# Alternating the forgetting and stick-breaking head pairs of a hybrid block on one Trainium2 core

## The chip, the core and the metric

One of the eight cores of a Trainium2 chip. The time is the device time of one execution in microseconds; several executions are timed and the median is taken. The engines are named as the profile names them: PE (TensorE; PEld its weight loads), DVE (VectorE), ACT (ScalarE), POOL (GpSimd) and SP (SyncE, whose queue issues most of the DMAs here).

## What is computed

Two transformer blocks on one sequence of 512 tokens (528 with 16 meta tokens), model width 1024, float32. The change lies in the mixer of the first block. Cut to it:

```python
proj = xn @ w_in[layer]
q_a, k_a, v_a, f_a, q_b, k_b, v_b, g_a, g_b = jnp.split(proj, SPLIT_POINTS, axis=-1)
log_f = jax.nn.log_sigmoid(f_a + b_forget[layer])
o_a = forgetting_attention(q_a, k_a, v_a, log_f)      # softmax(q k^T / 8 + c[t] - c[s]), c = cumsum(log f)
o_b = stick_breaking_attention(q_b, k_b, v_b)         # exp(log_sigmoid(z) + later), s < t
y_a = merge(o_a) @ w_o_fox[layer]
y_b = merge(o_b) @ w_o_sb[layer]
mixed = (jax.nn.sigmoid(g_a) * y_a + jax.nn.sigmoid(g_b) * y_b) @ w_out[layer]
h = h + rms_norm(mixed, norm_gains[layer, 1])
```

Here `later` is the sum of log_sigmoid(-z) over the keys between s and t, taken as a reversed cumulative sum. Each of the two attentions has eight heads of width 64; they are worked on in pairs, four pairs of either kind. Then come the first block's feed-forward part and a second block, whose ada rows (`silu(c) @ w_ada`) are already begun in the first mixer.

## The kernel before, in words

Every float32 product is made of three matmuls: both operands are split in a high and a low part of type fp32r, and `mm3` (L95 to L106) adds high × high (L102), low × high (L105) and high × low (L106). A weight tile is 128 × 512 (256 KB): SP loads it (`wr`), ACT copies it to its high part `wh` (L90), DVE subtracts to get the low part `wl` (L91). `dense` runs one weight key's column tile of 128 columns over the sequence in two halves (about 258 or 264 columns); a tile over 8 k tiles takes 48 matmuls, one over 4 takes 24.

`attention(fam, pr, pf)` is one pair, fam 0 forgetting, fam 1 stick-breaking. It projects q, k and v (three column tiles of `w_qkv`, 144 matmuls), forms scores in five query blocks (block 0 of 2 rows, blocks 4 to 1 of 128; L388 to L394), and turns them into weights P. For a forgetting pair that is a maximum on DVE and one Exp on ACT per block (`fox_rows`). For a stick-breaking pair ACT copies the scores to P (L400), and `sb_rows` runs a chain per block in a wide buffer `sb_l`: Abs, Exp and Ln on ACT, L565 on DVE (max and add), two reversed scans on DVE (L568), a subtraction on DVE (L569), and Exp on ACT. Then PE transposes P (L411), ACT and DVE split the transposed piece (`pt_h` L73, `pt_l` L74), and three matmuls add it to the bank `o` (L418 to L420). The meta keys go through `ptm` (L426 to L436). A forgetting pair divides by its sums (`rt` transposes L445, `rs` L449 to L452); both kinds are split to `o_h`, `o_l`.

The order of work: the program gives all instructions in one order, and a scheduler with a modelled timeline sets from it the order on each engine. Buffers and their numbers decide how far work can run ahead: the weight buffers (4 and 6), two P of each block, two `sb_l`, three banks for scores, one bank for `o`. In the program the forgetting pairs 0 to 3 come first, each followed by two column tiles of the gate projection `w_g` (`gate_a`). Then Silu of the condition, its store by SP, Sigmoid over all eight gated tiles `ya` (L501) and the table load that sets ACT back to Exp and Ln (L502). Then stick-breaking pairs 0 to 3 with no, one, one and six column tiles of `w_of` (the forgetting output projection, `out_a`, 24 matmuls each) behind them. Behind the pairs come eight gate tiles more (`sg`) with two ada rows each (`ada`: SP loads `wa`, 512 KB, L812; DVE multiplies it with the condition `wc` and sums, L813; `wc` itself is loaded at L802 from the stored condition), then `out_b` (`w_os`, L536 multiplies with the gate, POOL adds, the sum is split to `mix_h` and `mix_l`), whose first halves meet the `w_out` projection of the next stage.

Of the kernel before, what the change touches and what calls it, by code (L numbers as in the profile page):

```python
# [19 lines left out]
NT = 528  # L20
# [18 lines left out]
class Kernel:  # L39
# [21 lines left out]
        (eng or self.G).dma_start(out=t, in_=self.A[key])  # L61
        return t

    def load_r(self, p, key, shape, eng=None, dma=None):

        raw = self.load(p, key, shape, dma)
        t = p.tile(shape, F32R, name=key + "r", tag=key + "r")
        (eng or self.G).tensor_copy(t, raw)
        return t

    def split(self, h, l, src, scale=None, eng=None):
# [109 lines left out]
    def run(self):  # L181
        tc, nc = self.tc, self.nc
        top = ExitStack()
        nc.scalar.preload_act_table_set("natural_log_exp_and_others")
        const = self.const = self.pool(top, "const", side="left")
        self.wp = self.pool(top, "wp", bufs=4, side="left")
        self.wq = self.pool(top, "wq", bufs=6, side="left")
        self.gains1 = const.tile([128, 4, 8], F32, name="gains1")
        nc.sync.dma_start(out=self.gains1, in_=self.A["gains1"])
        self.ident = self.load(const, "ident", [128, 128])  # L190
        self.ones = const.tile([128, 1], F32, name="ones")
        self.V.memset(self.ones, 1.0)
        self.c15 = const.tile([128, 1], F32, name="c15")
        self.V.memset(self.c15, 1.5)
        self.zero = const.tile([128, 1], F32, name="zero")
        self.V.memset(self.zero, 0.0)
        self.gains2 = self.load(const, "gains2", [128, 3, 8])
        self.convw = self.load(const, "convw", [128, 44, 4])
        self.b_ada = self.load(const, "b_ada", [128, 48])
        self.mod = const.tile([128, 48], F32, name="mod")  # L200
        self.cond = self.load(const, "cT", [128, 8])
        self.cond_out = self.pool(top, "pdr", space=bass.MemoryType.DRAM).tile([128, 8], F32, name="cond")
        self.n_ada = 0
        xp = self.pool(top, "xp", side="left")
        self.xres = xp.tile([128, 8, NQ], F32, name="xres")
        self.x = self.xres[:, :, 2:NQ]
        self.block1_mixer()
        self.block1_ffn()
        self.block2_mixer()
        self.block2_ffn()  # L210
        top.close()


    def block1_mixer(self):
# [89 lines left out]
        def attention(fam, pr, pf):  # L304
# [59 lines left out]
            vtm = pa.tile([128, 2, 16], F32, tag="vtm", name="vtm")  # L364
            G.tensor_copy(vtm, vt[:, 0:16].unsqueeze(1).to_broadcast([128, 2, 16]))
            tr(tm, vtm.rearrange("p e s -> p (e s)"), ident)
            vmf = pa.tile([32, 128], F32, tag="vmf", name="vmf")
            V.tensor_tensor(vmf, tm, bmask, op=ALU.mult)
            for r in (0, 32):
                act(vm[z][r:r + 32], vmf, AF.Copy)  # L370
# [7 lines left out]
            for b in (0, 4, 3, 2, 1):  # L378
                t0, qn = QB[b]
                n = 16 + 128 * b  # L380
                qs = slice(t0 - T0, t0 - T0 + qn)
                pieces = [(0, n)] if n <= 512 else [(0, 264), (264, 264)]
                for e in range(2):
                    pss = []
                    for c0, cn in pieces:
                        ps = ps_s.tile([128, 512], F32, tag="s", name="s")[0:qn, 0:cn]
                        keys = ks[e][:, c0:c0 + cn]
                        mm(ps, qhh[e][:, qs], keys, start=True, stop=False)  # L388
                        if c0 + cn == n:
                            if b == 0:  # L390
                                mm(ps, self.ident_r[:, 0:2], mr[:, 128:144], start=False, stop=False)
                            else:
                                mm(ps[:, cn - 128:cn], self.ident_r, mr[:, 0:128], start=False, stop=False)
                        mm(ps, qll[e][:, qs], ks2[e][:, c0:c0 + cn], start=False, stop=True)  # L394
                        pss.append((ps, c0, cn))
                    if fam == 0:
                        self.fox_rows(pa2, pss, P[b], e, b, qn, sums)
                    else:
                        for ps, c0, cn in pss:
                            act(P[b][:, e, c0:c0 + cn], ps, AF.Copy)  # L400
                if fam == 1:
                    self.sb_rows(pf, P[b], qn, n)

            o = ps_o.tile([128, 512], F32, tag="o", name="o")
            first = True
# [31 lines left out]
            if fam == 0:  # L437
# [7 lines left out]
                    tr(rt[:, 128 * b - 128:128 * b], rx[:, b, :], ident)  # L445
                rt0 = ps_t.tile([128, 512], F32, tag="t", name="rt0")[:, 0:2]
                tr(rt0, rx[0:2, 0, :], ident[0:2, 0:2])
                rs = pf["pool"].tile([128, NQ], F32, tag="rs", name="rs")
                act(rs[:, 2:NQ], rt, AF.Copy)  # L449
                act(rs[:, 0:2], rt0, AF.Copy)  # L450
                V.tensor_tensor(rs[:, 2:NQ], o, rs[:, 2:NQ], op=ALU.mult)
# [11 lines left out]
        c8 = kc[1]  # L463
        G.memset(c8[0:64].bitcast(F32), 0.0)
        y = pa.tile([8, NT], F32, tag="vt", name="fy")
        l = pf.tile([8, NT], F32, tag="rs", name="fl")
        late = []
        dense("w_f", 0, xn_h, xn_l, 0, KD,
              lambda ps, c0, n: V.tensor_tensor(y[:, c0:c0 + n], ps[0:8], rb[0:8, c0:c0 + n], op=ALU.mult),
# [20 lines left out]
        def out_a(ps, c0, n, i):  # L490
            V.tensor_tensor(ya[:, i, c0:c0 + n], ps, ya[:, i, c0:c0 + n], op=ALU.mult)

        for pr in range(4):
            attention(0, pr, fox)
            for i in (2 * pr, 2 * pr + 1):
                dense("w_g", i, xn_h, xn_l, T0, QD, lambda ps, c0, n: gate_a(ps, c0, n, i))
        self.dump("o0", o_h[0])
        esf.close()
        self.tc.keep_in_program_order(act(self.cond, self.cond, AF.Silu))
        nc.sync.dma_start(out=self.cond_out, in_=self.cond)  # L500
        act(ya, ya, AF.Sigmoid)  # L501
        tables = nc.scalar.preload_act_table_set("natural_log_exp_and_others")  # L502
        self.tc.keep_in_program_order(tables)


        ess = ExitStack()
        psb = self.pool(ess, "psb", bufs=2)
        sb = {"pool": psb, "tables": tables.ins}
        for pr in range(4):
            attention(1, pr, sb)  # L510
            for i in [[], [0], [1], range(2, 8)][pr]:
                dense("w_of", i, o_h[0], o_l[0], 0, QD, lambda ps, c0, n: out_a(ps, c0, n, i))
        self.dump("o1", o_h[1])
        ess.close()
        esa.close()
        esp.close()

# [36 lines left out]
            self.act(P[:, e, c0:c0 + cn], ps, AF.Exp, bias=nm[0:qn, 0:1], accum_out=s2[0:qn, i:i + 1])  # L554
        V.tensor_tensor(sums[0:qn, e, b:b + 1], s2[0:qn, 0:1], s2[0:qn, 1:2], op=ALU.add)

    def sb_rows(self, pf, P, qn, n):

        V, act = self.V, self.act
        l = pf["pool"].tile([128, 2, NT], F32, tag="sb_l", name="sb_l")[0:qn, :, 0:n]  # L560
        with self.tc.issue_after(pf["tables"]):
            act(l, P, AF.Abs)
            act(l, l, AF.Exp, scale=-1.0)
            act(l, l, AF.Ln, bias=self.ones[0:qn])
        V.scalar_tensor_tensor(l, P, 0.0, l, op0=ALU.max, op1=ALU.add)  # L565
        for e in range(2):
            r = l[:, e, ::-1]
            V.tensor_tensor_scan(r, r, self.zero[0:qn].to_broadcast([qn, n]), 0.0, op0=ALU.add, op1=ALU.add)  # L568
        V.tensor_tensor(P, P, l, op=ALU.subtract)  # L569
        act(P, P, AF.Exp)  # L570
# [249 lines left out]
    def block2_mixer(self):  # L820
# [7 lines left out]
        nm = py.tile([128, S], F32R, name="nm")  # L828
        ut = py.tile([128, 4, 36], F32, name="ut")
        fl = py.tile([128, 2, 4, 4], F32, name="fl")  # L830
        sel = self.load_r(py, "lsel", [128, 8], dma=nc.sync)
        mk = [self.load(py, f"lmask{d}", [128, 128], nc.sync) for d in range(2)]
        ng = self.load(py, "mng", [128, 4], nc.sync)
        pcv = self.pool(es_c, "pcv", side="left")
# [618 lines left out]
```

## Time and profile before

| what | value |
|---|---|
| runs | 1557.49, 1564.07, 1560.18 us; median 1560.18 us |
| profiled execution | 1563.27 us, its span 1561.5 us |
| mean granted clock of TensorE | 0.982 |
| PE, DVE, ACT, POOL busy | 96%, 66%, 53%, 11% of the span |
| instructions in the span | 27525 |
| first mixer's head pairs | from about 50 to 370 us of the span |

How to read it: an engine is busy while it executes an instruction; the granted clock is the share of full speed that TensorE was given, so a busy us at 0.5 does half a us of full-speed work. Starts and ends are us from the start of the span. In a timeline the bracket behind a row holds the idle time of that engine just before it and the instruction whose end released it. The span is 1.8 us shorter than the time of the same execution.

### The profile page before, as it was taken

What the parts mean: (1) busy time and instruction counts of PE and PEld (TensorE: products, weight loads), DVE (VectorE), ACT (ScalarE), POOL (GpSimd) and SP (SyncE); (2) the same over time, 40 slices, a digit from 0 to 9 for tenths busy, and PEclk for the clock granted to TensorE, in tenths of its full rate; (3) what the DMA queues carried; (4) which work ended last, traced back from release to release, by engine and by line L of the source; (5) the groups of instructions that cost most, each with busy time, mean ns of one, the idle gap of its engine ahead of it and who ended that gap; (6) DMA issues with size and microseconds to landing.
All of it is one profiled execution on the core that took longest, in us unless ns stands there. A gap on an engine that the chain in (4) does not pass through costs nothing. (4 is left out here: it accounts for less than half of the span.)

```text
span 1561.5 us, 27525 instructions
## 1 busy us (share of the span) xinstructions
PE 1499.8 (96%) x10219; PEld 1366.8 (88%) x10219; DVE 1031.0 (66%) x2052; ACT 821.0 (53%) x1704; POOL 177.6 (11%) x290
## 2 busy tenths in 40 slices
PE   7999998999899899999999999999998999999997
PEld 6999997889899899999899997775788888888887
DVE  7666568875978997787546877656878633333335
ACT  5455667774367654444345666767455433333232
POOL 4000000000234200000002213321331000000000
PEclk9999998999999999999999999999999999999998
DMA  6322232114864544444556653210135633333334
GB/s 190 93 75 86 62 95 75 48 55 143 278 218 139 172 147 139 138 136 121 180 162 173 188 178 116 68 55 0 36 122 177 215 95 95 95 94 88 93 101 138
DMA packets 101510, 190.43 MB, mean 122 GB/s; under 512 B 12480, under 2 KB 19840, under 8 KB 101376
## 3 DMA queue, kind: packets, MB, share of 16 engines
q1 hardware_dynamic: 100432, 187.26, 38.9%
q0 software_dynamic: 944, 1.41, 0.4%
q8 instruction: 80, 1.31, 0.4%
q14 instruction: 54, 0.44, 0.1%
HBM read 181.63 MB, written 2.10 MB: 118 GB/s over the span
## 5 line engine op out<-in xcount | busy, mean ns | idle before, releaser
L91 DVE TENSOR_TENSOR wl<-wr,wh 128x512 fp32r<-128x512 f32 x576 | 401.8, 703 | 285.2 <-ACT wh L90 274.3
L90 ACT ACTIVATE wh<-wr 128x512 fp32r<-128x512 f32 x576 | 355.8, 621 | 437.1 <-PE d L105 312.0
L102 PE MATMUL d<-x_h,wh 128*128 128x258 f32 (+1 forms) x704 | 198.5, 282 | 1.8 <-DVE ev L676 1.7
L106 PE MATMUL d<-x_h,wl 128*128 128x258 f32 (+1 forms) x704 | 198.2, 282 | 0.8 <-DVE wl L91 0.8
L105 PE MATMUL d<-x_l,wh 128*128 128x258 f32 (+1 forms) x704 | 198.8, 283 | 0.0
L102 PE MATMUL d<-xn_h,wh 128*128 128x264 f32 (+2 forms) x656 | 189.4, 290 | 8.2 <-ACT xn_h L247 6.4
L105 PE MATMUL d<-xn_l,wh 128*128 128x264 f32 (+2 forms) x656 | 189.6, 289 | 1.8 <-DVE xn_l L248 1.8
L106 PE MATMUL d<-xn_h,wl 128*128 128x264 f32 (+2 forms) x656 | 189.2, 289 | 0.0
L106 PE MATMUL d<-g_h,wl 128*128 128x256 f32 (+1 forms) x506 | 163.8, 324 | 0.0
L102 PE MATMUL d<-g_h,wh 128*128 128x256 f32 (+1 forms) x506 | 163.6, 323 | 0.0
L105 PE MATMUL d<-g_l,wh 128*128 128x256 f32 (+1 forms) x506 | 163.5, 323 | 0.0
L105 PE MATMUL d<-f_l,wh 128*128 128x512 f32 (+1 forms) x416 | 149.4, 363 | 2.9 <-DVE f_l L796 2.9
L106 PE MATMUL d<-f_h,wl 128*128 128x512 f32 (+1 forms) x416 | 149.1, 362 | 0.0
L102 PE MATMUL d<-f_h,wh 128*128 128x512 f32 (+1 forms) x416 | 146.6, 361 | 1.5 <-ACT f_h L795 1.0
L102 PEld LDWEIGHTS d<-x_h,wh 128*128 128x128 f32 x704 | 132.9, 189 | 2.6 <-DVE ev L676 2.3
L102 PEld LDWEIGHTS d<-xn_h,wh 128*128 128x128 f32 x656 | 125.8, 193 | 9.3 <-ACT xn_h L247 6.7
L106 PEld LDWEIGHTS d<-x_h,wl 128*128 128x128 f32 x704 | 132.8, 189 | 1.0 <-DVE wl L91 1.0
L105 PEld LDWEIGHTS d<-x_l,wh 128*128 128x128 f32 x704 | 132.6, 189 | 0.1
L105 PEld LDWEIGHTS d<-xn_l,wh 128*128 128x128 f32 x656 | 126.1, 192 | 3.3 <-DVE xn_l L248 3.1
L106 PEld LDWEIGHTS d<-xn_h,wl 128*128 128x128 f32 x656 | 126.0, 192 | 0.5 <-DVE wl L91 0.2
L105 PEld LDWEIGHTS d<-g_l,wh 128*128 128x128 f32 x506 | 95.0, 188 | 8.6
L102 PEld LDWEIGHTS d<-g_h,wh 128*128 128x128 f32 x506 | 95.1, 188 | 8.1
(514 smaller groups left out, 3298.2 us busy)
## 6 DMA issues: line engine op xcount, KB each, us to landing
wr<-in_w_down SPq DMA_DIRECT2D x115, 256.0 KB, 2.8
wr<-in_w_up SPq DMA_DIRECT2D x104, 256.0 KB, 2.7
wr<-in_w_gu SPq DMA_DIRECT2D x104, 256.0 KB, 2.6
wa<-in_w_ada SPq DMA_DIRECT2D x48, 512.0 KB, 4.5
wr<-in_w_in SPq DMA_DIRECT2D x68, 256.0 KB, 2.9
wr<-in_w_out SPq DMA_DIRECT2D x56, 256.0 KB, 2.9
wr<-in_w_qkv SPq DMA_DIRECT2D x48, 256.0 KB, 2.7
wr<-in_w_g SPq DMA_DIRECT2D x32, 256.0 KB, 2.6
```

The lines of the kernel that those rows point to most:

```text
L90: self.act(wh, raw, AF.Copy)
L91: eng.tensor_tensor(wl, raw, wh.bitcast(F32), op=ALU.subtract)
L102: m = self.mm(ps, wh[:, k, :], h, start=(j == 0 and k == 0), stop=False)
L105: self.mm(ps, wh[:, k, :], xl[:, k0 + k, c0:c0 + n], start=False, stop=False)
L106: self.mm(ps, wl[:, k, :], h, start=False, stop=(j == last and k == kt - 1))
```

## The change

The two kinds of pair take turns: forgetting 0, stick-breaking 0, forgetting 1 and so on. The gate tiles of `ya` stand behind the stick-breaking pairs, three, three, two and none. All eight `w_of` tiles come behind the last pair. Silu, the store of the condition, Sigmoid and the table load stand between forgetting pair 3 and stick-breaking pair 3. So that both kinds' buffers fit at once, the pool of the wide buffer has two tags of one buffer (528 wide for blocks 4 and 2, 400 wide for the others) in place of two equal ones, and `vmf`, `rs` and `l` are put into other tiles. `load_r` has POOL's queue load straight into the fp32r tile, with no raw tile and no cast. The table set that the program begins with now serves the stick-breaking pairs up to the third.

```diff
--- before.py
+++ after.py
@@ -61,11 +61,10 @@
         (eng or self.G).dma_start(out=t, in_=self.A[key])
         return t
 
-    def load_r(self, p, key, shape, eng=None, dma=None):
-
-        raw = self.load(p, key, shape, dma)
+    def load_r(self, p, key, shape):
+
         t = p.tile(shape, F32R, name=key + "r", tag=key + "r")
-        (eng or self.G).tensor_copy(t, raw)
+        self.G.dma_start(out=t, in_=self.A[key])
         return t
 
     def split(self, h, l, src, scale=None, eng=None):
@@ -181,7 +180,7 @@
     def run(self):
         tc, nc = self.tc, self.nc
         top = ExitStack()
-        nc.scalar.preload_act_table_set("natural_log_exp_and_others")
+        self.tables = nc.scalar.preload_act_table_set("natural_log_exp_and_others")
         const = self.const = self.pool(top, "const", side="left")
         self.wp = self.pool(top, "wp", bufs=4, side="left")
         self.wq = self.pool(top, "wq", bufs=6, side="left")
@@ -364,7 +363,7 @@
             vtm = pa.tile([128, 2, 16], F32, tag="vtm", name="vtm")
             G.tensor_copy(vtm, vt[:, 0:16].unsqueeze(1).to_broadcast([128, 2, 16]))
             tr(tm, vtm.rearrange("p e s -> p (e s)"), ident)
-            vmf = pa.tile([32, 128], F32, tag="vmf", name="vmf")
+            vmf = vt[0:32, 16:144]
             V.tensor_tensor(vmf, tm, bmask, op=ALU.mult)
             for r in (0, 32):
                 act(vm[z][r:r + 32], vmf, AF.Copy)
@@ -399,7 +398,7 @@
                         for ps, c0, cn in pss:
                             act(P[b][:, e, c0:c0 + cn], ps, AF.Copy)
                 if fam == 1:
-                    self.sb_rows(pf, P[b], qn, n)
+                    self.sb_rows(pf, P[b], b, qn, n)
 
             o = ps_o.tile([128, 512], F32, tag="o", name="o")
             first = True
@@ -445,7 +444,7 @@
                     tr(rt[:, 128 * b - 128:128 * b], rx[:, b, :], ident)
                 rt0 = ps_t.tile([128, 512], F32, tag="t", name="rt0")[:, 0:2]
                 tr(rt0, rx[0:2, 0, :], ident[0:2, 0:2])
-                rs = pf["pool"].tile([128, NQ], F32, tag="rs", name="rs")
+                rs = pa2.tile([128, NT], F32, tag="pt_h", name="rs")[:, 0:NQ]
                 act(rs[:, 2:NQ], rt, AF.Copy)
                 act(rs[:, 0:2], rt0, AF.Copy)
                 V.tensor_tensor(rs[:, 2:NQ], o, rs[:, 2:NQ], op=ALU.mult)
@@ -463,7 +462,7 @@
         c8 = kc[1]
         G.memset(c8[0:64].bitcast(F32), 0.0)
         y = pa.tile([8, NT], F32, tag="vt", name="fy")
-        l = pf.tile([8, NT], F32, tag="rs", name="fl")
+        l = pa2.tile([8, NT], F32, tag="pt_h", name="fl")
         late = []
         dense("w_f", 0, xn_h, xn_l, 0, KD,
               lambda ps, c0, n: V.tensor_tensor(y[:, c0:c0 + n], ps[0:8], rb[0:8, c0:c0 + n], op=ALU.mult),
@@ -490,28 +489,29 @@
         def out_a(ps, c0, n, i):
             V.tensor_tensor(ya[:, i, c0:c0 + n], ps, ya[:, i, c0:c0 + n], op=ALU.mult)
 
+
+        ess = ExitStack()
+        sb = {"tables": self.tables.ins}
         for pr in range(4):
             attention(0, pr, fox)
-            for i in (2 * pr, 2 * pr + 1):
+            if pr == 0:
+                sb["pool"] = self.pool(ess, "psb")
+            if pr == 3:
+                self.tc.keep_in_program_order(act(self.cond, self.cond, AF.Silu))
+                nc.sync.dma_start(out=self.cond_out, in_=self.cond)
+                act(ya, ya, AF.Sigmoid)
+                tables = nc.scalar.preload_act_table_set("natural_log_exp_and_others")
+                self.tc.keep_in_program_order(tables)
+                sb["tables"] = tables.ins
+            attention(1, pr, sb)
+            for i in [(0, 1, 2), (3, 4, 5), (6, 7), ()][pr]:
                 dense("w_g", i, xn_h, xn_l, T0, QD, lambda ps, c0, n: gate_a(ps, c0, n, i))
+        for i in range(8):
+            dense("w_of", i, o_h[0], o_l[0], 0, QD, lambda ps, c0, n: out_a(ps, c0, n, i))
         self.dump("o0", o_h[0])
-        esf.close()
-        self.tc.keep_in_program_order(act(self.cond, self.cond, AF.Silu))
-        nc.sync.dma_start(out=self.cond_out, in_=self.cond)
-        act(ya, ya, AF.Sigmoid)
-        tables = nc.scalar.preload_act_table_set("natural_log_exp_and_others")
-        self.tc.keep_in_program_order(tables)
-
-
-        ess = ExitStack()
-        psb = self.pool(ess, "psb", bufs=2)
-        sb = {"pool": psb, "tables": tables.ins}
-        for pr in range(4):
-            attention(1, pr, sb)
-            for i in [[], [0], [1], range(2, 8)][pr]:
-                dense("w_of", i, o_h[0], o_l[0], 0, QD, lambda ps, c0, n: out_a(ps, c0, n, i))
         self.dump("o1", o_h[1])
         ess.close()
+        esf.close()
         esa.close()
         esp.close()
 
@@ -554,10 +554,10 @@
             self.act(P[:, e, c0:c0 + cn], ps, AF.Exp, bias=nm[0:qn, 0:1], accum_out=s2[0:qn, i:i + 1])
         V.tensor_tensor(sums[0:qn, e, b:b + 1], s2[0:qn, 0:1], s2[0:qn, 1:2], op=ALU.add)
 
-    def sb_rows(self, pf, P, qn, n):
+    def sb_rows(self, pf, P, b, qn, n):
 
         V, act = self.V, self.act
-        l = pf["pool"].tile([128, 2, NT], F32, tag="sb_l", name="sb_l")[0:qn, :, 0:n]
+        l = pf["pool"].tile([128, 2, NT - 128 * (b % 2 == 1 or b == 0)], F32, tag=f"sb_l{b in (4, 2)}", name="sb_l")[0:qn, :, 0:n]
         with self.tc.issue_after(pf["tables"]):
             act(l, P, AF.Abs)
             act(l, l, AF.Exp, scale=-1.0)
@@ -828,7 +828,7 @@
         nm = py.tile([128, S], F32R, name="nm")
         ut = py.tile([128, 4, 36], F32, name="ut")
         fl = py.tile([128, 2, 4, 4], F32, name="fl")
-        sel = self.load_r(py, "lsel", [128, 8], dma=nc.sync)
+        sel = self.load_r(py, "lsel", [128, 8])
         mk = [self.load(py, f"lmask{d}", [128, 128], nc.sync) for d in range(2)]
         ng = self.load(py, "mng", [128, 4], nc.sync)
         pcv = self.pool(es_c, "pcv", side="left")
```

How instructions move on PE around stick-breaking pair 0, where its products `o` are formed (`xn_h`, `xn_l`, `wh`, `wl` are those of a projection, `P` the pair's weights). Before:

```order
L418 MATMUL o<-pt_h,vp_h_208 128x512
L419 MATMUL o<-pt_l,vp_h_208 128x512
L420 MATMUL o<-pt_h,vp_l_210 128x512
L418 MATMUL o<-pt_h,vp_h_208 128x384
L411 MATMUL pt<-ident,P_2915 128x128
L411 MATMUL pt<-ident,P_2916 128x128
L419 MATMUL o<-pt_l,vp_h_208 128x384
L420 MATMUL o<-pt_h,vp_l_210 128x384
```

and in the change:

```order
L101 MATMUL d<-xn_h,wh 128x264
L417 MATMUL o<-pt_h,vp_h_204 128x512
L104 MATMUL d<-xn_l,wh 128x264
L105 MATMUL d<-xn_h,wl 128x264
L101 MATMUL d<-xn_h,wh 128x264
L104 MATMUL d<-xn_l,wh 128x264
L105 MATMUL d<-xn_h,wl 128x264
L387 MATMUL s<-ks,qhh 2x16
L390 MATMUL s<-mask0r,ident_r 2x16
L418 MATMUL o<-pt_l,vp_h_204 128x512
```

Between the products of the pair there now stand the projections of forgetting pair 1 and that pair's first scores (`mask0r` is the forgetting mask). Lines of the changed kernel are lower by one there.

PE at the end of forgetting pair 3. Before:

```order
L434 MATMUL o<-ptm,vm_213 128x512
L436 MATMUL o_2517<-ptm,vm_213 128x2
L445 MATMUL rt<-ident,rx 128x128 x4
L394 MATMUL s<-ks,qll 128x272
L388 MATMUL s<-ks,qhh 128x144
L393 MATMUL s<-mask1r,ident_r 128x128
L394 MATMUL s<-ks,qll 128x144
L388 MATMUL s<-ks,qhh 128x144
L393 MATMUL s<-mask1r,ident_r 128x128
L394 MATMUL s<-ks,qll 128x144
L106 MATMUL d<-xn_h,wl 128x264
L102 MATMUL d<-xn_h,wh 128x264
```

and in the change:

```order
L433 MATMUL o<-ptm,vm_209 128x512
L435 MATMUL o_4005<-ptm,vm_209 128x2
L444 MATMUL rt<-ident,rx 128x128 x4
L446 MATMUL rt_4016<-ident,rx 128x2
L358 MATMUL tv<-ident,vt 128x128 x4
L365 MATMUL tm<-ident,vtm 32x128
L101 MATMUL d<-o_h_94,wh 128x258
L101 MATMUL d<-o_h_94,wh 128x256
L104 MATMUL d<-o_l_96,wh 128x258
L105 MATMUL d<-o_h_94,wl 128x258
L104 MATMUL d<-o_l_96,wh 128x256
L105 MATMUL d<-o_h_94,wl 128x256
```

Behind forgetting pair 3 there were the scores and projections of stick-breaking pairs; now there is the first `w_of` tile's last k tile, which reads this pair's `o_h` and `o_l`. On DVE the same place now reads (`sb_l` and `P` are those of stick-breaking pair 3, `ptm`, `rs` and `o_l` those of forgetting pair 3):

```order
L568 SCALAR_TENSOR_TENSOR sb_l<-sb_l,zero 128x272 x2
L569 TENSOR_TENSOR P_4269<-P_4269,sb_l 128x544
L565 SCALAR_TENSOR_TENSOR sb_l<-P_4268,sb_l 128x2x144
L568 SCALAR_TENSOR_TENSOR sb_l<-sb_l,zero 128x144 x2
L569 TENSOR_TENSOR P_4268<-P_4268,sb_l 128x288
L432 TENSOR_TENSOR ptm<-ptm 32x512
L432 TENSOR_TENSOR ptm<-ptm_3996,ptm 32x2
L450 TENSOR_TENSOR rs<-o,rs 128x512
L451 TENSOR_TENSOR rs<-o_4005,rs 128x2
L73 TENSOR_TENSOR o_l_96<-rs,o_h_94 128x514
```

The last steps of forgetting pair 3 stand behind the chain of stick-breaking pair 3.

DVE at `w_os`, behind the mixer's gate tiles. Before:

```order
L813 SCALAR_TENSOR_TENSOR wa,mod<-wa,wc 128x1024
L536 TENSOR_TENSOR sg<-d,sg 128x258
L91 TENSOR_TENSOR wl<-wr,wh 128x512
L817 TENSOR_TENSOR mod<-mod,b_ada 128x2
L536 TENSOR_TENSOR sg<-d,sg 128x258
L813 SCALAR_TENSOR_TENSOR wa,mod<-wa,wc 128x1024
L91 TENSOR_TENSOR wl<-wr,wh 128x512
L536 TENSOR_TENSOR sg<-d,sg 128x258
L74 TENSOR_TENSOR mix_l<-sg,mix_h 128x258
L813 SCALAR_TENSOR_TENSOR wa,mod<-wa,wc 128x1024
L74 TENSOR_TENSOR mix_l<-sg,mix_h 128x258
```

and in the change:

```order
L528 TENSOR_TENSOR sg<-d,rb 128x256
L90 TENSOR_TENSOR wl<-wr,wh 128x512
L536 TENSOR_TENSOR sg<-d,sg 128x258
L90 TENSOR_TENSOR wl<-wr,wh 128x512
L536 TENSOR_TENSOR sg<-d,sg 128x258
L90 TENSOR_TENSOR wl<-wr,wh 128x512
L73 TENSOR_TENSOR mix_l<-sg,mix_h 128x258
L536 TENSOR_TENSOR sg<-d,sg 128x258
L90 TENSOR_TENSOR wl<-wr,wh 128x512
L73 TENSOR_TENSOR mix_l<-sg,mix_h 128x258
```

The ada multiplies (L813) that stood among the `w_os` multiplies (L536) now all stand ahead of them.

## Rows read from the trace of the kernel before

**Rows 1.** Part 1 of the page: busy us, share of the span, instructions.
```profile
PE 1499.8 (96%) x10219; PEld 1366.8 (88%) x10219; DVE 1031.0 (66%) x2052; ACT 821.0 (53%) x1704; POOL 177.6 (11%) x290
```

**Rows 2.** Windows: stretch, us; busy PE, PEld, DVE, ACT, POOL; granted clock, DMA share, GB/s.
```profile
100.00:120.00 20.00, 20.00 (x165) 19.73 (x165) 14.73 (x34) 12.28 (x31) 1.69 (x3) 1.00 0.33 95
260.00:280.00 20.00, 11.56 (x49) 9.35 (x49) 16.03 (x27) 12.02 (x31) 0.00 (x0) 0.66 0.09 27
280.00:300.00 20.00, 20.00 (x150) 19.77 (x151) 15.84 (x30) 17.26 (x34) 0.21 (x1) 0.91 0.09 29
300.00:320.00 20.00, 18.02 (x127) 17.15 (x125) 15.69 (x37) 14.36 (x36) 0.00 (x0) 0.86 0.33 92
320.00:380.00 60.00, 58.41 (x463) 55.85 (x462) 39.47 (x79) 35.21 (x71) 0.21 (x1) 0.99 0.22 66
400.00:420.00 20.00, 16.74 (x132) 15.79 (x131) 19.23 (x38) 7.22 (x14) 5.32 (x5) 1.00 0.86 297
420.00:440.00 20.00, 18.97 (x134) 18.55 (x135) 15.30 (x29) 11.84 (x26) 4.14 (x5) 0.83 0.65 209
```

**Rows 3.** Timeline of PE: start us, us, line, operands [idle before <- releaser].
```profile
257.51 0.17 PE L388 MATMUL s<-ks,qhh 128*2 128x16 f32 x1
...
277.46 0.59 PE L388 MATMUL s<-ks,qhh 128*128 128x264 f32 x1 [2.27 <-ACT P L400]
...
283.18 0.42 PE L102 MATMUL d<-o_h,wh 128*128 128x258 f32 x1
...
314.57 0.59 PE L388 MATMUL s<-ks,qhh 128*128 128x264 f32 x1 [1.74 <-ACT P L400]
```

**Rows 4.** Timeline of DVE, 259 to 290 us.
```profile
259.12 1.26 DVE L565 SCALAR_TENSOR_TENSOR sb_l<-P,sb_l 128x1056 f32<-128x1056 f32 x1 [0.29 <-ACT sb_l L564]
...
275.98 0.46 DVE L569 TENSOR_TENSOR P<-P,sb_l 128x288 f32<-128x288 f32 x1
...
288.00 1.26 DVE L565 SCALAR_TENSOR_TENSOR sb_l<-P,sb_l 128x1056 f32<-128x1056 f32 x1 [0.38 <-ACT sb_l L564]
```

**Rows 5.** Timeline of DVE at the seam, 405 to 425 us.
```profile
414.18 1.77 DVE L813 SCALAR_TENSOR_TENSOR wa<-wa,wc 128x1024 f32<-128x1024 f32 x1
```

**Rows 6.** Timeline of PE at the seam, 412 to 424 us.
```profile
420.76 0.58 PE L105 MATMUL d<-mix_l,wh 128*128 128x258 f32 x1 [1.44 <-DVE mix_l L74]
```

**Rows 7.** DVE by line, 257 to 284 us: count, busy us, mean ns, idle before.
```profile
L568 DVE TENSOR_TENSOR_SCAN sb_l<-sb_l,zero 128x528 f32<-128x528 f32 (+4 forms) x10 | 6.7, 708 | 0.0
L74 DVE TENSOR_TENSOR pt_l<-pt,pt_h 128x512 fp32r<-128x512 f32 (+3 forms) x8 | 3.6, 487 | 1.3 <-ACT pt_h L73 1.3
L569 DVE TENSOR_TENSOR P<-P,sb_l 128x1056 f32<-128x1056 f32 (+4 forms) x5 | 3.6, 718 | 0.1
L565 DVE SCALAR_TENSOR_TENSOR sb_l<-P,sb_l 128x1056 f32<-128x1056 f32 (+4 forms) x5 | 3.6, 713 | 3.0 <-ACT sb_l L564 3.0
```

**Rows 8.** Timeline of DVE, 205 to 226 us, the end of forgetting pair 3.
```profile
215.60 0.68 DVE L433 TENSOR_TENSOR ptm<-ptm 32x512 fp32r<-32x512 f32 x1 [1.65 <-PE s L394]
...
220.41 0.69 DVE L451 TENSOR_TENSOR rs<-o,rs 128x512 f32<-128x512 f32 x1 [0.17 <-ACT rs L449]
...
224.88 0.69 DVE L74 TENSOR_TENSOR o_l<-rs,o_h 128x514 fp32r<-128x514 f32 x1 [0.22 <-ACT o_h L73]
```

**Rows 9.** DVE by line and form, 0 to 480 us.
```profile
L91 DVE TENSOR_TENSOR wl<-wr,wh 128x512 fp32r<-128x512 f32 x136 | 98.6, 728 | 35.3 <-ACT wh L90 32.4 <-PE d L106 1.7
...
L74 DVE TENSOR_TENSOR mix_l<-sg,mix_h 128x258 fp32r<-128x258 f32 x8 | 4.6, 573 | 0.0
...
L536 DVE TENSOR_TENSOR sg<-d,sg 128x256 f32<-128x256 f32 x8 | 3.3, 415 | 0.2 <-PE d L106 0.2
```

**Rows 10.** Timeline of SP, 365 to 415 us.
```profile
377.60 2.08 SPq L812 DMA_DIRECT2D wa<-in_w_ada  x3
```

**Rows 11.** Timeline of ACT, 183 to 194 us.
```profile
186.40 1.28 ACT L501 ACT_TABLE_LOAD   x1
187.69 3.65 ACT L501 ACTIVATE xres<-xres 128x4112 f32<-128x4112 f32 x1
```

## The prediction

> **What bounds the kernel now.** I read the busy times first: PE works 96% of the span, DVE 66%, ACT 53%, POOL 11% [rows 1]. Matmuls are not changed by the edit, so it can only win or lose PE time that is idle or slow. I therefore went through the windows of the first mixer [rows 2] and charged each with "lost" time: what PE is idle, plus (1 − granted clock) × what it is busy. The reader is to see three things there. In the forgetting stage (100–120 is one of ten such windows) nothing is lost. Around stick-breaking pair 0, 260–280 loses 8.44 + 0.34 × 11.56 = 12.4 us and 280–300 loses 1.8; 300–320 loses 1.98 + 0.14 × 18.02 = 4.5; 320–380 loses 2.2. At the end of the mixer 400–420 loses 3.3 and 420–440 1.0 + 0.17 × 18.97 = 4.2. Together 28.4 us.
>
> Then the PE timeline, for why [rows 3]. At 257.51 the projections of the moment are done and PE has only pair 0's scores, transposes and products; the next projection-like matmul (w_of) starts at 283.18. For 25.7 us PE waits on the chain of pair 0 on ACT and DVE, at the last 2.27 us for a score copy that frees a bank. The DVE timeline shows the chain [rows 4]: 17.3 us from the first L565 (259.12) to the end of the last wide L569 (276.44). This I call **stretch A**. Its own work at full clock is the window 257.5–283.2 less its loss: about 25.8 − 14 = 11.8 us.
>
> The third loss is the seam w_os → w_out. DVE is busy 19.23 of 20 us there; L813 multiplies of the ada rows, up to 1.77 us each, stand between the multiplies that feed mix_l, and PE waits 1.44 us for mix_l at 420.76 [rows 2, 5, 6].
>
> **The change part by part.**
>
> *1. Alternating pairs.* The order on PE shows that groups of three projection matmuls now stand between pair 0's products, where before there was nothing. Whether this covers the chain is a sum. PE: a pair's q, k, v are 144 matmuls at 0.12 us (165 in the full 20 us of 100–120 [rows 2]), 17.3 us, and with A's 11.8 that is 29.1. DVE: 13.9 in L565, L568 and L569, 3.6 in pt_l, some 2.1 in ptm, vp_l and o_l (0.7 each, as ptm and o_l of a forgetting pair), six wl of 0.728, six evictions taken as L536's 0.415, and eight q and k subtractions at no more than that [rows 7 to 9]: 17.5 + 2.1 + 4.4 + 2.5 + 3.3 = 30 at most. So the two are even before a gate tile is counted; three tiles add 17.3 us to PE and some 7 to DVE. With gates DVE is the shorter, so stretch A goes, and the 4.5 + 2.2 of 300–380 shrink to some 2 (turns between pairs still cost a little): **−4.7** for that part; bounds −6.7 (nothing is lost) and 0.
>
> *2. A new stretch B at the end.* All w_of tiles need o_h of all four forgetting pairs, and forgetting pair 3 now ends late. On DVE its ptm, rs and o_l stand behind the whole chain of stick-breaking pair 3; on PE, between the last q, k, v matmul and the first use of its o_h, only 18 w_of matmuls (the first three k tiles of tile 0, two halves: 18 × 0.12 = 2.2 us) are there as cover. So A is not removed but moved. Its length: a lead from the first scores to the first L565 of about 9 (288.00 − 277.46 = 10.5 for pair 1 [rows 3, 4]); a DVE chain of 15 (17.3 less two wl of 0.73 and two pt_l of 0.49 that lay inside [rows 4, 7, 9]); a tail of 5 (forgetting pair 3 now: 0.68 ptm, 0.69 rs, 0.69 o_l with the ACT steps and transposes between [rows 8]). Together 29. Work for PE in it: A's 11.8 + 0.8 more scores + 0.7 more transposes + 0.5 for rt and tm + 2.2 w_of = 16. Lost 13, plus 1.5 at a low clock afterwards (1.8 after A) = 14.5, against 14 to 14.2 for A: **+0.5**. Bounds: if only DVE work counts (13.9 + 3.6 + 0.8 + 0.7 + 0.7 = 20 us [rows 7, 8]) B loses 4 to 6.5 us, −7.5; with a lead of 10.5, a chain of 17.3 and a wait of a few us between fox and sb steps it is 37 long, +8. I take the middle because the rows of A, the nearest ones, already hold ACT's part of the lead.
>
> *3. The ada rows.* wc (L802) now waits in SP's queue for pair 3's last transposes, before the 73 remaining w_of matmuls, not after them; the ada loads start some 9 us before the gate stage, where now they start with it (377.60 [rows 10]). On DVE all sixteen L813 stand ahead of the first L536; before, four stood among the L536. Then each first half of a w_os tile costs DVE 0.415 (L536) + 0.728 (wl) + 0.573 (mix_l) [rows 9], eight of them 13.7 us, against 8 × 12 × 0.12 = 11.5 us of PE. That leaves 2.2, and with the last half's way through mix_h and mix_l, some 1.3, the seam still loses 3.5 of 7.5: **−4**. Bounds 0 and −7.5. The loads have time if they run at today's rate: 13 MB (wc twice, sixteen rows of 512 KB, w_g) at the 297 GB/s of 400–420 [rows 2] is 44 us; the 9 us and eight gate tiles of 48 × 0.12 = 5.8 us make 55.
>
> *4. Small edits, taken at nothing.* Masks and lsel by POOL's queue without casts: POOL is 11% busy, and the first mask is used at the first scores. One table load fewer (1.28 us of ACT [rows 11], which is 53% busy). rs, l and vmf in other tiles; the wide buffer by size, two slots as before. SP's wait of the cond store for Silu: nothing queued behind it is needed earlier. If the cover were gone, each costs under 1.3 us.
>
> One place needs more: Sigmoid over ya and two table loads now stand in ACT's queue in the middle of stick-breaking pair 2's chain. They take 1.28 + 3.65 + 1.28 = 6.2 us, and the load runs into Sigmoid without a gap (186.40 + 1.28 → 187.69) [rows 11]. With some 22 other ACT steps of 0.48 us (821.0 / 1704 [rows 1]) that is 16.8 us, under the 17.3 us of projections that PE has then. No wait, by 0.5 us. The Trainium skill, "ScalarE: Activation LUTs", section "What ACT_TABLE_LOAD costs", adds about 1.4 us of drain to the 1283 ns of each load. By that estimate two loads make ACT 2.8 us longer, PE waits 2.3 us, and the sum would be near −6 in place of −8. The trace agrees with the 1.28 and shows no drain; I go by the trace.
>
> **Sum.** −4.7 + 0.5 − 4 = −8.2. The profiled execution took 1563.27 us (span 1561.5), 3.1 above the median of 1560.18; so 1555.1 against its own time, and **1552.0** against the median.
>
> **Rivals.**
> *Stretch B is only as long as its DVE work* (gain). Forgetting pair 3's steps slip into ACT waits of the chain (3.0 us of idle before L565 in A [rows 7]), and B loses 7.5 less than A: −16.2, 1544. For: DVE idles in A. Against: the order puts the tail behind the chain. Chance 0.18.
> *The seam stays.* Ada rows and w_g share the transfers; below 240 GB/s (13 MB in 55 us) rows come late, and their L813, now in front, hold up the multiplies behind them. −4 is lost, or a little more: about 1557. For: the DMA engines are 0.86 busy in 400–420 [rows 2]. Against: 297 GB/s there. Chance 0.15.
> *Slower: each turn stalls.* In 300–320 stick-breaking scores wait 1.74 us for ACT's score copy (314.57 [rows 3]), the clock falls, and 4.5 us are lost. Six new turns between pairs of different kind come up (three each way). Two such losses eat the gain; four make +18 − 8.2: 1570; all six 1579. For: ACT order is shared by two chains. Against: the transposes and gates lie beside. Chance 0.13.
> Anything else, slower: 0.04. That the change does not do what it says is not open for the order, which shows it.
>
> **How the numbers follow.** My case 0.50, own range 1548 to 1556. A measurement of this kernel tells about 0.5%, 7.8 us, from no change: faster means under 1552.4, slower over 1568. My case gives 0.28 faster and 0.22 same; the first rival 0.18 faster; the second 0.02 and 0.13; the third 0.04 same and 0.09 slower; the rest 0.04 slower: 0.48, 0.39, 0.13. The range leaves out the slower two (about 0.15) and the extreme of the first: 1542 to 1565.
>
> **What would show it.** Right: no window of the interleaved stretch loses over 1 us; one stretch near its end, some 29 us from the last v matmul to the first w_of matmul with forgetting pair 3's o_h, loses 13 to 15; wc lands before the gate stage; no L813 after the first L536; PE waits at the seam fall by half. Wrong: losses of 2 us or more at the turns with ACT as releaser; a B under 22 us; L813 waiting for DMA late in the gate stage.

## The result and the profile after

The changed kernel takes 1547.32 us (median of 4, 1547.08 to 1547.67), the kernel before 1561.22 in the same comparison: ratio 0.9913 with a 95% interval of 0.9898 to 0.9927, some 14 us. A second measurement gave 0.9917 (0.9902 to 0.9933). The forecast was 1552.0, 8.2 us down; the range 1542 to 1565 held the time, and the gain is larger than forecast.

The profiled execution took 1547.16 us, its span is 1545.4. Part 1 of the page, against [rows 1]:

```profile
PE 1490.3 (96%) x10219; PEld 1359.0 (88%) x10219; DVE 1033.0 (67%) x2052; ACT 817.5 (53%) x1703; POOL 177.6 (11%) x288
```

The same matmuls; PE is 9.5 us less busy, at a mean granted clock of 0.987 against 0.982. Now the windows, with the columns of [rows 2]; "lost" is again idle PE time plus (1 − clock) × busy.

```profile
60.00:260.00 200.00, 200.00 (x1646) 195.41 (x1645) 145.67 (x311) 143.38 (x334) 6.17 (x14) 1.00 0.28 79
260.00:295.00 35.00, 33.35 (x267) 31.64 (x267) 25.27 (x62) 23.26 (x71) 1.14 (x3) 1.00 0.30 83
295.00:325.00 30.00, 21.73 (x114) 17.81 (x113) 21.42 (x41) 22.30 (x45) 0.00 (x0) 0.72 0.03 9
325.00:382.00 57.00, 57.00 (x473) 56.23 (x472) 40.10 (x87) 18.25 (x34) 0.00 (x0) 1.00 0.69 236
382.00:430.00 48.00, 47.83 (x398) 47.42 (x397) 34.18 (x59) 27.10 (x55) 9.61 (x10) 1.00 0.59 182
```

- 60–260, now with three stick-breaking chains begun inside it, loses nothing. 260–295 loses 1.65. The 14.2 of stretch A and the 6.7 of 300–380 [rows 2] have no counterpart in these two windows.
- 295–325 is stretch B: 8.27 idle + 0.28 × 21.73 = 14.35 us, in the place of A's 14.2.
- 382–430 holds w_os and its seam: 0.17 us lost, where 7.5 were.

Stretch B on PE, the counterpart of A in [rows 3]:

```profile
291.01 0.28 PE L105 MATMUL d<-xn_h,wl 128*128 128x264 f32 x1
...
306.05 0.50 PE L418 MATMUL o<-pt_l,vp_h 128*128 128x512 f32 x1 [2.27 <-DVE pt_l L73]
...
310.29 0.58 PE L418 MATMUL o<-pt_l,vp_h 128*128 128x256 f32 x1 [1.76 <-DVE pt_l L73]
...
314.97 0.80 PE L433 MATMUL o<-ptm,vm 128*128 128x512 f32 x1 [1.64 <-DVE ptm L432]
...
318.93 0.78 PE L101 MATMUL d<-o_h,wh 128*128 128x258 f32 x2
```

PE waits 2.27 and 1.76 us for pt_l and 1.64 for ptm, 5.67 of the 8.27 us of idle time; the rest are shorter waits for ACT. The last projection matmul (291.01) ends at 291.29, and at 318.93 w_of meets forgetting pair 3's o_h: B is 27.6 us long. On DVE those pt_l and ptm stand between the steps of stick-breaking pair 3's chain, behind scans and subtractions of the chain:

```profile
299.09 1.26 DVE L565 SCALAR_TENSOR_TENSOR sb_l<-P,sb_l 128x1056 f32<-128x1056 f32 x1 [3.37 <-ACT sb_l L564]
...
303.23 1.26 DVE L569 TENSOR_TENSOR P<-P,sb_l 128x1056 f32<-128x1056 f32 x1
...
305.31 1.15 DVE L73 TENSOR_TENSOR pt_l<-pt,pt_h 128x512 fp32r<-128x512 f32 x2
306.37 1.86 DVE L568 TENSOR_TENSOR_SCAN sb_l<-sb_l,zero 128x400 f32<-128x400 f32 x2
...
313.68 0.46 DVE L569 TENSOR_TENSOR P<-P,sb_l 128x288 f32<-128x288 f32 x1
314.23 0.68 DVE L432 TENSOR_TENSOR ptm<-ptm 32x512 fp32r<-32x512 f32 x1
```

The seam on DVE, against [rows 5]: the last L813 ends 12.6 us ahead of the first L536, and that L536 waits for PE, not PE for it.

```profile
383.39 1.22 DVE L813 SCALAR_TENSOR_TENSOR wa<-wa,wc 128x1024 f32<-128x1024 f32 x1
...
397.20 0.43 DVE L536 TENSOR_TENSOR sg<-d,sg 128x258 f32<-128x258 f32 x1 [0.16 <-PE d L105]
...
399.91 0.97 DVE L73 TENSOR_TENSOR mix_l<-sg,mix_h 128x258 fp32r<-128x258 f32 x1
```

ACT around Sigmoid, against [rows 11]:

```profile
243.24 1.28 ACT L502 ACT_TABLE_LOAD   x1
244.53 3.64 ACT L502 ACTIVATE xres<-xres 128x4112 f32<-128x4112 f32 x1
248.19 1.28 ACT L503 ACT_TABLE_LOAD   x1
```

The loads take 1.28 us and Sigmoid starts 0.01 us behind the first; PE, beside it, does not wait once between 222 and 250. The drain of about 1.4 us that the Trainium skill, "ScalarE: Activation LUTs", section "What ACT_TABLE_LOAD costs", adds is not to be seen here either.

A part is given back outside the mixer. At the next stage's seam PE waits for a small reciprocal-root chain on POOL: 2.03 us before, where the granted clock stays at 1.00 (525–540), and 2.83 now, where the clock is 0.50 in 520–524. The first row is of before, the second of the changed kernel:

```profile
533.00 0.43 PE L156 MATMUL rb<-ident,rs_y 128*128 128x128 f32 x2 [2.03 <-POOL rs_y L141]
```

```profile
518.39 0.43 PE L155 MATMUL rb<-ident,rs_y 128*128 128x128 f32 x2 [2.83 <-POOL rs_y L140]
```

With the clock that is 6.3 us lost in 510–526, against 3.0 in 530–535 before.

### The profile page after: what moved, and what is told of

It is laid out like the page before. It is cut to its first block, busy times and chain, and to the rows that moved or that the text cites. A ratio compares the mean times of both kernels' runs of the same rounds, so it can differ in the third digit from the quotient of the medians.

```text
span 1545.4 us, 27524 instructions
## 1 busy us (share of the span) xinstructions
PE 1490.3 (96%) x10219; PEld 1359.0 (88%) x10219; DVE 1033.0 (67%) x2052; ACT 817.5 (53%) x1703; POOL 177.6 (11%) x288
```

## The experiments

Lost times are of each one's profiled execution; all are compared with the kernel before on the same chip, whose medians lay between 1561.1 and 1562.4.

**1. early_f3: is B there because w_of lacks forgetting pair 3's o_h?**

```diff
-        for pr in range(4):
-            attention(0, pr, fox)
...
+        for fam, pr in ((0, 0), (1, 0), (0, 1), (1, 1), (0, 2), (0, 3), (1, 2), (1, 3)):
...
-            attention(1, pr, sb)
...
+            attention(fam, pr, sb if fam else fox)
```

The gate tiles stand behind stick-breaking 0 (0 to 2), stick-breaking 1 (3 to 5) and forgetting 3 (6, 7).

> The changed kernel with forgetting pair 3 ahead of stick-breaking pair 2, so that the last two pairs are stick-breaking ones and all w_of inputs are ready before the last chain. Theory (stretch B, which lost 14.6 us in the changed kernel, exists because w_of needs forgetting pair 3's o_h): B goes, PE has w_of matmuls beside the chains, and the time falls by 10 to 14 us below the changed kernel's 1547.3, to 1533 to 1537. Rival (the chain itself is the limit, DVE and ACT can't feed PE there whatever it has to do): two stick-breaking pairs in a row lose as before, time within 4 us of 1547.

Measured 1538.0 us, ratio 0.9844 (0.9821 to 0.9868). Its windows:

```profile
60.00:285.00 225.00, 225.00 (x1846) 219.71 (x1845) 160.29 (x350) 158.79 (x381) 7.14 (x16) 1.00 0.27 79
285.00:330.00 45.00, 40.64 (x323) 38.10 (x323) 39.15 (x80) 34.83 (x75) 0.21 (x1) 1.00 0.19 60
380.00:410.00 30.00, 29.75 (x248) 29.47 (x247) 25.86 (x46) 15.60 (x33) 7.83 (x8) 1.00 0.68 218
```

The last two chains, 285–330, lose 4.4 us where the changed kernel loses 14.35 in B alone, and the clock stays at 1.00. w_of matmuls stand beside the chains now. The gain over the changed kernel is 9 to 10 us, a little under the 10 to 14 that were expected; the theory holds. This version beats both kernels.

**2. b_small: the small edits alone**, on the kernel before.

```diff
+        self.G.dma_start(out=t, in_=self.A[key])
...
+            vmf = vt[0:32, 16:144]
...
-        psb = self.pool(ess, "psb", bufs=2)
+        psb = self.pool(ess, "psb")
```

> The kernel before with the small edits alone (masks and lsel by POOL's queue without casts, vmf, rs and l in other tiles, wide buffer by size), order of the pairs unchanged. Theory (they cost and bring nothing): 1560 to 1562, within 2 us of before. Rival (a part of the gain of 14 comes from them, the first 60 us of the changed kernel lost 1.1 us less): 1555 to 1558.

Measured 1559.65, ratio 0.999 (0.9976 to 1.0003). The interval holds no change; up to 3.7 us of gain are not excluded, so they are at most some quarter of the 14. In the profiled execution PE is idle for 62.5 us of the span (1554.5 less 1492.0 busy), in the kernel before for 61.7 (1561.5 less 1499.8). What differs between the two is the mean granted clock, 0.990 against 0.982, not the waiting.

**3. b_rows12, a_rows12: the seam without L813 among L536.** The same edit on the kernel before and on the changed one:

```diff
-            self.ada(2)
+            self.ada(2 if i < 6 else 0)
...
-            self.ada(1 if f < 20 else 0)
+            self.ada((2 if f < 8 else 1) if f < 20 else 0)
```

> The kernel before with twelve ada rows in the mixer in place of sixteen; the other four go to the next stage's up projection, so that no L813 stands among the L536. Theory (the seam's 7.5 us are the four multiplies in DVE's queue): the seam's loss falls below 1 us and the time by 5 to 7, to 1554 to 1556, less what the four rows cost later (0 to 1). Rival (the seam waits because DVE is short of time for w_os in any case, 13.7 us against 11.5 of PE): 3.5 us or more remain, time 1557 to 1560.

> The same edit on the changed kernel, where no L813 stood among the L536 already. Theory: nothing to win at the seam, 1546 to 1549. Rival (the rows share transfers with the weights in the gate stage and slow it): 1542 to 1545.

b_rows12: 1558.85, ratio 0.9989 (0.9975 to 1.0003), against the theory. Its timelines of DVE and PE at the seam, and the window:

```profile
405.07 1.22 DVE L813 SCALAR_TENSOR_TENSOR wa<-wa,wc 128x1024 f32<-128x1024 f32 x1
406.22 0.09 DVE L813 DVE_READ_ACCUMULATOR wa<-wa,wc 128x1 f32 x1
406.22 0.43 DVE L536 TENSOR_TENSOR sg<-d,sg 128x258 f32<-128x258 f32 x1
```

```profile
413.07 0.39 PE L105 MATMUL d<-mix_l,wh 128*128 128x258 f32 x1 [0.31 <-DVE mix_l L74]
...
414.88 0.39 PE L105 MATMUL d<-mix_l,wh 128*128 128x258 f32 x1 [1.18 <-DVE mix_l L74]
...
416.68 0.58 PE L105 MATMUL d<-mix_l,wh 128*128 128x258 f32 x1 [1.06 <-DVE mix_l L74]
```

```profile
410.00:425.00 15.00, 12.27 (x75) 11.47 (x74) 12.58 (x21) 7.51 (x17) 5.55 (x6) 0.77 0.69 225
```

No L813 stands among the L536, yet PE still waits for mix_l three times. 410–425 loses 5.55 us and the 10 us ahead of it 0.12, so only 1.8 of 7.5 are won. DVE comes to the first L536 straight from an L813, 6.9 us after PE's first w_os matmul (399.30); in the changed kernel that is 1.65 us (395.55 to 397.20). a_rows12: 1548.36, ratio 0.9923 (0.9905 to 0.994), the changed kernel's time; there was nothing to win.

**4. b_rows8: eight rows fewer, to tell lateness from shortage.** As above with `i < 4` and `f < 12`.

> The kernel before with eight ada rows in the mixer; the other eight go to the next stage's up projection. With twelve rows the last L813 ran until 406.2, the first L536 came at 406.22, 6 us behind PE's first w_os matmuls, and the seam still lost 5.7 of 7.5 us. Theory (what the seam loses is DVE's lateness at its start, made by the rows that arrive late and hold up the queue, not the four multiplies among the L536 alone): the last L813 ends some 10 us before the first L536, the seam loses under 1.5 us, time 5 to 7 below before. Rival (DVE is too short at w_os in any case, 1.82 us a tile against PE's 1.44): 4 us or more remain lost, within 4 us of before.

Measured 1554.5, ratio 0.995 (0.9932 to 0.9967): 7.3 us. The window of its seam:

```profile
395.00:425.00 30.00, 29.88 (x248) 29.47 (x247) 26.42 (x48) 17.96 (x36) 8.08 (x8) 1.00 0.69 213
```

0.12 us lost, although DVE spends the same 1.82 us a tile there (the L536 of 406.84 to 415.95 come at that distance) against PE's 1.44 (12 matmuls of 0.12). The first L536 comes 1.65 us after the first w_os matmul (401.62 to 403.27). DVE is not too slow at the seam; it came late to it. The other profiles say the same. Where the first L536 comes 6.3 to 7.1 us behind the first w_os matmul (the kernel before, b_rows12 and, below, fox_first and early_f3b), the seam loses 3.2 to 7.5 us. Where it comes 1.6 to 2.1 us behind (the changed kernel, a_rows12, b_rows8, early_f3, and below alt_only and early_f3_rows12), it loses 0.12 to 0.25. How PE gets over the 0.38 us by which DVE is slower per tile was not singled out; the five banks for `d` there (pool `ps_f`) are a likely reason.

**5. fox_first: are gate tiles enough to cover the chain?** All forgetting pairs first, the gate tiles as in the changed kernel; Silu and Sigmoid come behind stick-breaking pair 2's last Exp here:

```diff
+        gates = {(1, 0): (0, 1, 2), (1, 1): (3, 4, 5), (1, 2): (6, 7)}
+        for fam, pr in ((0, 0), (0, 1), (0, 2), (0, 3), (1, 0), (1, 1), (1, 2), (1, 3)):
...
+                with self.tc.issue_after(self.last_exp):
```

> The changed kernel, but all forgetting pairs first as in the kernel before; the gate tiles stay behind stick-breaking pairs 0 to 2, w_of behind the last, and Silu and Sigmoid come behind pair 2's last Exp. Theory (stretch A needs matmuls beside the chain, whichever; three gate tiles are 17.3 us for its 14 us of loss): A falls below 3 us without any alternation, B does not come up since all w_of inputs are ready, time 1536 to 1542. Rival (the alternation itself is what covers the chain, gate tiles come too late or DVE is full): A keeps 7 us or more, 1545 to 1553.

Measured 1545.18, ratio 0.9892 (0.9871 to 0.9912), above the expected stretch but faster than the kernel before by 16.6 us with no alternation at all. Windows:

```profile
60.00:170.00 110.00, 106.14 (x852) 101.26 (x851) 70.88 (x181) 71.22 (x207) 6.46 (x12) 1.00 0.25 73
170.00:285.00 115.00, 115.00 (x948) 112.47 (x947) 88.31 (x168) 79.73 (x170) 0.42 (x2) 1.00 0.25 74
285.00:330.00 45.00, 42.25 (x324) 40.05 (x324) 35.44 (x72) 37.86 (x72) 0.21 (x1) 0.96 0.27 76
385.00:410.00 25.00, 21.49 (x167) 20.18 (x166) 23.90 (x47) 10.06 (x20) 7.06 (x7) 1.00 0.74 241
```

A is gone as expected: 170–285, where the chains of pairs 0 and 1 run (their wide L565 at 169.49 and 219.03), loses nothing; 285–330 loses 4.4 us. But 60–170, the forgetting stage that gave its gate tiles away, now loses 3.9, and the seam 3.5, since the ada rows come late again (ada multiplies among those of w_os until 399.29). The theory holds for A; the time missed for two reasons that it left out.

**6. alt_only: is the alternation enough without gate tiles?** Tiles 2·pr and 2·pr + 1 stand behind forgetting pair pr again:

```diff
+            for i in (2 * pr, 2 * pr + 1):
+                dense("w_g", i, xn_h, xn_l, T0, QD, lambda ps, c0, n: gate_a(ps, c0, n, i))
...
             attention(1, pr, sb)
-            for i in [(0, 1, 2), (3, 4, 5), (6, 7), ()][pr]:
...
```

> The changed kernel with the gate tiles behind the forgetting pairs again, two each, so that the alternation stands alone (Silu and Sigmoid behind stick-breaking pair 2's last Exp, one table load more). Theory (the sum of the prediction: the next forgetting pair's q, k and v are 17.3 us, with the pair's own 11.8 it is 29.1 of PE against 30 of DVE, so alternation alone is just even): stretches of the first three chains lose 2 to 6 us in all where the changed kernel loses 1.9; B and the seam as in the changed kernel; 1547 to 1552. Rival (gate tiles are what covers the chains, as in fox_first, and alternation brings nothing of it): 8 us or more lost, 1554 to 1560.

Measured 1566.69, ratio 1.0048 (1.0029 to 1.0066): slower than the kernel before, which neither side expected. The windows of the three turns from a stick-breaking to a forgetting pair, then PE and DVE in the first:

```profile
105.00:120.00 15.00, 8.94 (x60) 8.15 (x58) 12.67 (x31) 8.27 (x22) 0.21 (x1) 0.77 0.28 73
185.00:200.00 15.00, 9.70 (x61) 8.75 (x60) 11.50 (x30) 7.25 (x21) 0.21 (x1) 0.77 0.26 86
265.00:280.00 15.00, 9.71 (x62) 8.69 (x60) 10.84 (x29) 8.00 (x22) 0.21 (x1) 0.77 0.20 59
```

```profile
108.38 0.40 PE L393 MATMUL s<-kc,qll 128*2 128x16 f32 x3
111.95 0.39 PE L387 MATMUL s<-ks,qhh 128*128 128x264 f32 x1 [3.17 <-ACT P L550]
...
113.26 0.59 PE L387 MATMUL s<-ks,qhh 128*128 128x264 f32 x1 [0.69 <-ACT P L550]
```

```profile
111.35 0.15 DVE L548 TENSOR_REDUCE nm<-s 2x1 f32<-2x16 f32 x1
111.43 1.32 DVE L569 TENSOR_TENSOR_SCAN sb_l<-sb_l,zero 128x272 f32<-128x272 f32 x2
112.68 0.14 DVE L548 TENSOR_REDUCE nm<-s 2x1 f32<-2x16 f32 x1
```

Each turn loses 7.5 to 8.1 us, 23 in all; with 13.6 in 300–400, where B lies, that is some 37 us against 28.4 in the kernel before, and the time rose by 5.6. The forgetting pair's first scores fill the score banks at 108.4. Their maxima (L548 in this kernel) stand in DVE's queue behind steps of the chain and other pieces, with DVE busy for 12.67 of the window's 15 us: the first comes at 111.35, the second at 112.68, behind two scans. ACT's Exp waits for them, PE waits 3.17 us for Exp and, at 116.27, another 2.20 for DVE to take v out of its bank, and the granted clock falls (0.77 in the window). The sum that set 29.1 us of PE against 30 of DVE counted amounts and was silent on order. In the changed kernel three gate tiles stand at the first two turns and nothing is lost there; two stand at the third, and 1.65 us are lost.

**7. early_f3b and early_f3_rows12: more from the better order?** The first has two gate tiles behind each of stick-breaking 0 and 1, forgetting 3 and stick-breaking 2, with Sigmoid behind pair 2's last Exp; the second is early_f3 with the edit of experiment 3.

> As early_f3 (1538.0), with two gate tiles behind each of stick-breaking 0 and 1, forgetting 3 and stick-breaking 2, and Silu and Sigmoid behind pair 2's last Exp, so that ACT changes tables three times in one place. Theory (in early_f3 4.6 us are still lost between 60 and 430 us, 1.8 of them at 290 where cover is thin): more cover late brings 1 to 3 us, 1535 to 1537. Rival (the last losses are steps that no cover reaches): within 1.5 us of 1538, or worse by the 3.6 us that Sigmoid holds up ACT in the last chain.

> early_f3 with twelve ada rows in the mixer. Its seam lost 0.25 us, with the last L813 just ahead of the second L536. Theory (DVE's lateness decides, and there is little of it here): within 2 us of early_f3, 1536 to 1539. Rival (the 2 to 3 us that early_f3 loses after the changed kernel between 430 and 460 us come from that lateness too): 1534 to 1536.

early_f3b: 1542.62, ratio 0.9872 (0.9852 to 0.9892), slower than early_f3 and above the 1535 to 1537 expected: its seam lost 3.2 us, as the ada rows came later (the second load of wc at 354.06, in early_f3 at 343.91) and two L813 stood among the L536 again. early_f3_rows12: 1537.17, ratio 0.9848 (0.9828 to 0.9867), the same as early_f3 within the intervals.

**8. after_again: the changed kernel beside the last three.**

> The changed kernel once more, beside the others on the same chip. Expected 1546 to 1549; every theory says the same, it gives the distance to early_f3 on one chip.

Measured 1547.8, ratio 0.9917, as expected; early_f3_rows12 is 10.6 us below it on one chip.

## Why the prediction was right, and where it was off

*Step 1, alternation, −4.7:* measured 6.7 − 1.65: −5.0. The number was right in part by luck, for its reason was half right. The prediction let the next pair's projections carry the cover and the gate tiles come on top. fox_first shows that gate tiles alone remove A, and alt_only that without them each turn costs 7.5 to 8.1 us. So it is the place of the gate tiles, not the alternation itself, that covers the chains. The rival "each turn stalls" described a real mechanism, with DVE's maxima in the place of ACT's score copy, and priced it too low at 4.5; in the changed kernel the gate tiles keep it away. The sign that no window of the interleaved stretch loses over 1 us was missed by a little: the third turn loses 1.65.

The prediction's reading of A was also off by a pair. Rows of the kernel before, first on DVE, then on PE:

```profile
231.78 1.26 DVE L565 SCALAR_TENSOR_TENSOR sb_l<-P,sb_l 128x1056 f32<-128x1056 f32 x1
...
264.70 0.62 DVE L74 TENSOR_TENSOR pt_l<-pt,pt_h 128x256 fp32r<-128x256 f32 x2
```

```profile
265.17 0.58 PE L419 MATMUL o<-pt_l,vp_h 128*128 128x256 f32 x1 [3.49 <-DVE pt_l L74]
```

Each pair has one wide L565 of 128x1056, and they start at 231.78, 259.12, 288.00 and 325.31. So the chain at 259.12 is that of pair 1, the products of 258 to 275 are pair 0's, and the scores at 257.51 and 277.46 pair 2's. Pair 0's own chain ran from 231.78 beside projections and cost nothing. In A, PE waits longest (3.49 us) for a small split of pair 0's products that stands behind steps of pair 1's chain on DVE. That is B's mechanism too, with forgetting pair 3 in the place of pair 0.

*Step 2, stretch B, +0.5:* measured 14.35 against 14.2. Right in place, size and cause: forgetting pair 3's steps behind the chain on DVE, 18 w_of matmuls as cover; early_f3 removes it by giving w_of its inputs. The parts of its length were right as well: 8.0 us from the first scores (291.13) to the wide L565 (299.09), 15.1 of chain (to 314.14) and 4.8 of tail (to 318.93), against 9, 15 and 5. The rival of a B of 20 us fell.

*Step 3, the ada rows, −4:* this is the term that was mis-sized; it measured −7.3. The prediction had the four L813 among the L536 as the cause and kept 3.5 us because DVE's 13.7 us exceed PE's 11.5. The runs show both to be wrong readings. The four multiplies are worth 1.8 (b_rows12); DVE's excess costs next to nothing when it starts level (b_rows8, 0.12 lost; after, 0.17). What costs is that the rows come late and keep DVE busy into the seam. Fewer rows are fewer transfers too, but the DMA share of 395–425 is nearly the same in b_rows8 (0.69) and b_rows12 (0.72), so transfers are the less likely reason; no run separates the two. The prediction saw only the wait for mix_l. In the kernel before more of PE's idle time at the seam, 2.54 of 4.29 us, is spent waiting for ACT's wh (two of three such waits on PE, then ACT):

```profile
414.07 0.36 PE L102 MATMUL d<-o_h,wh 128*128 128x258 f32 x1 [0.82 <-ACT wh L90]
...
416.78 0.36 PE L102 MATMUL d<-mix_h,wh 128*128 128x258 f32 x1 [1.02 <-ACT wh L90]
```

```profile
413.07 0.42 ACT L73 ACTIVATE mix_h<-sg 128x258 fp32r<-128x258 f32 x1 [1.67 <-POOL sg L537]
413.40 1.14 ACT L90 ACTIVATE wh<-wr 128x512 fp32r<-128x512 f32 x2
```

Two of the three wh stand in ACT's queue behind a mix_h that waits for POOL's add, which follows DVE's late L536; the third, of 416.08, waits 0.76 us for its own weight's transfer. The rows now start further ahead than reckoned: before, the first load (L812, 377.60) came 6.8 us behind the first gate tile's L528 at 370.77; now it comes 12.1 us ahead of it (343.15 and 355.29). That is 19 us, not 9. The transfer rival fell with it: the last L813 is done 12.6 us before the first L536.

*Step 4, small edits at nothing:* no change shown (b_small); the two table loads cost PE no wait.

*Sum:* −5.0 + 0.2 − 7.3 = −12.1. At the next stage's seam the two profiled executions stand 14.6 us apart (533.00 to 518.39). One us of this lies in the first 50 us (14.3 lost before, 13.3 now), but after_again lost 15.6 in its first 60, so it is not the change's. Behind that row the changed kernel loses 3 us more than the kernel before, and yet it ends 16.1 us ahead. So some 1.5 us ahead of the seam and 4 behind it have no name. Where the clock falls differs between executions of the same work: b_rows12 has the order of the kernel before up to the gate stage and lost 11.3 us in 260–300, where that kernel lost 14.2; and the clock was 0.89 in 1200–1215 of the kernel before, 1.00 at the same place in the changed one (1185–1200) and 0.89 again in after_again (1188–1203). The medians differ by 14. The kernel before scatters from 1556.45 to 1566.11 over all these runs and its profiled execution lay 2 us above its median, so what is unnamed was not settled; up to 3.7 us could be the small edits.

## What to carry to other kernels

Ask of filler work not only how much there is but whether it can be finished when the stall comes: gate tiles, which need no result of the chain, cover it; the next pair's projections end in scores whose maxima queue behind that chain. When an order moves a stall to the end of a stage, look which tiles behind it need only part of the inputs, and finish those inputs first. At a seam, look whether an engine arrives late before you count what it does there.

## What was not expected of the hardware

Elementwise times stretch beside POOL. In the changed kernel's seam mix_l takes 0.96 to 0.97 us wherever POOL's add (L537, 1.05 us) runs, and 0.41 at 412.33, when POOL is through. Not every overlap does it: the wl between them, which read two tiles as well and meet the start of the add, keep 0.67 to 0.68 us, but for one of 0.99 at 398.06. The small POOL steps of the reciprocal root, 128 × 2 elements each, took 0.19 to 1.85 us in one chain:

```profile
513.53 1.85 POOL L137 TENSOR_TENSOR rs_t<-rs_y 128x2 f32<-128x2 f32 x1
515.47 0.32 POOL L138 TENSOR_TENSOR rs_t<-rs_t,rs_v 128x2 f32<-128x2 f32 x1
...
518.14 0.20 POOL L140 TENSOR_TENSOR rs_y<-rs_y,rs_t 128x2 f32<-128x2 f32 x1
```

The Trainium skill, "GPSIMD Engine Reference", section "1. Specifications", says that POOL shares its SBUF interfaces with VectorE and contends with instructions that read two SBUF inputs. mix_l's rows agree, the wl rows only in part. For the POOL steps the partner was not singled out by a run. The chain took 7.5 us in the changed kernel (510.82 to 518.34), two steps of 1.52 and 1.85 among them, and 5.6 before (527.36 to 532.95), with none over 0.72. PE's wait for it is 2.8 to 2.9 us in the changed kernel, after_again, a_rows12, early_f3 and early_f3_rows12, but 1.85 in fox_first and 1.90 in early_f3b; why was not settled.
